# Mean over 8,192 rows: another cut of the last row group, of the early columns and of the third wide add

## The chip, the cores and the metric

The kernel runs on one core of one Trainium2 chip. The metric is the time of one execution on the device in microseconds (us), the median of several runs. A profile of one execution shows a span, from its first to its last instruction, which is somewhat shorter than that time.

## The reference

```python
def setup_inputs():
    return {"x": np.random.randn(8192, 8192).astype(np.float32)}

def reference(x):
    return np.mean(x, axis=0)
```

The input is 8,192 x 8,192 float32 values, 268 MB; the output is one row of 8,192 column means.

## The kernel before

**Row groups and strips.** The 8,192 rows are 64 groups of 128 rows, one row per SBUF partition. Since the order of rows does not matter to a sum, the groups are cut from four strips of x (`strips`, 17, 17, 15 and 15 groups), in which every partition holds consecutive rows. Two consecutive rows of a strip make a "pair", 64 KB in one run per partition, 8 MB in all; there are 30 pairs. Each strip leaves one single row group: r60, r61, r62 and r63.

**Loads.** SyncE issues every load (`load`, L52), in the order of the program. `bufs` has six slots of one row group each. Slots 4 and 5 are the accumulators `both` and `acc`: the first pair is loaded straight into them. Slots 0 to 3 take the other pairs in turn, two slots at a time (`u = (g + 2) % 4`, where g counts row groups). A load into a slot waits for the add that read the slot's earlier rows; SyncE stands at that load until then, and everything behind it stands too.

**Early columns.** A part of r60, its first six blocks of 512 columns, is loaded ahead into the tile `early` (`load_early`): two blocks as the first load of all, four blocks after the third pair. GpSimd adds them to `acc` in two instructions much later (L137, after g = 24 and g = 32), so that r60 itself is loaded without them.

**Adds.** VectorE does the summing (`add`, L80). For g = 2, 4 and 6 it does a wide add: a pair of rows is added to `both` and `acc` at once (16,384 columns). At g = 6 the wide add leaves out the first 1,024 columns of both rows (14,336 remain), and TensorE takes these instead in four products at L129, which start the accumulation in bank 0. Then `both` is added to `acc`, and from g = 8 on each pair takes two adds of 8,192: the pair's two rows into `both`, and `both` into `acc`. A no-op on ScalarE or GpSimd (L83) does each add's waiting for its load and the add ahead.

**The last groups.** VectorE adds columns 6 x 512 and up of r60 and r61, and columns 10 x 512 and up of r62, to `acc`. What is left is r61's blocks 0 to 5, r62's blocks 0 to 9, all of r63, and `acc`. These go to TensorE (`product`, L102), which multiplies each block with a column of 1/8192 and so sums over the 128 partitions. A block i of 512 columns goes to PSUM bank i // 4, column group q = i % 4 of TensorE (output partitions 32q to 32q + 31). The trace has two matmul records ("passes") for a product.

**The last quarter of the columns** (12 x 512 and up) is cut otherwise: `chunks` views its 2,048 columns as (j q w), so that a piece j holds a strip of each column group. r63 comes in four loads: blocks 0 to 7, 8 to 11, 12 to 14 and block 15 (j = 0 to 2, and j = 3). With W = 128, j = 0 to 2 make 384 columns per column group in bank 3, and j = 3 makes 128 columns in bank 4. Both the shares of `acc` and of r63 accumulate in the same bank.

**The order of the products** is the order of the list `sums`: acc 0-5, r61 0-5, r62 0-9, acc 6-7, r63 0-7, acc 8-11, r63 8-11, acc's pieces, r63's pieces. TensorE's waits come in this order.

**The output.** ScalarE copies banks 0, 1, 2 and 3 to SBUF (L182) and issues the first store, s0 (8 KB); SyncE issues s1 (16 KB, banks 1 and 2) and the last store (8 KB, tile `fin`, L199). VectorE copies bank 4 to `fin` (L192). SyncE's no-ops (`landed`, L47) wait for loads, stores and engines, since the program must not end ahead of them: some stand before s1, one before the last store, and the rest behind it.

Of the kernel before, what the change touches and what calls it, by code (L numbers as in the profile page):

```python
# [9 lines left out]
def kernel(  # L10
# [5 lines left out]
    nc = tc.nc  # L16
    f32 = mybir.dt.float32
    M, N = x.shape
    P = nc.NUM_PARTITIONS
    F = 512  # L20
    W = F // 4
    G = M // P
    U = 6
    sync = mybir.DependencyInfo(mybir.DependencyClass.Sync, mybir.DependencyReason.DATA)
# [2 lines left out]
    psp = ctx.enter_context(tc.tile_pool(name="psum", bufs=1, space=bass.MemoryType.PSUM))  # L27

    bufs = sb.tile([P, U, N], f32, name="bufs")
    both = bufs[:, U - 2, :]  # L30
    acc = bufs[:, U - 1, :]
    ones = sb.tile([P, 32], f32, name="ones")
    E = 6
    early = sb.tile([P, E * F], f32, name="early")
    fin = sb.tile([P, F], f32, name="fin")
# [2 lines left out]
    ready = sb.tile([P, 1], f32, name="ready")  # L38
    tc.keep_in_program_order(
        nc.gpsimd.tensor_add(out=ready[:], in0=ones[:, 0:1], in1=ones[:, 1:2]))  # L40
    banks = [psp.tile([P, F], f32, name=f"bank{b}") for b in range(5)]

    loads = []

    def landed(*inss):

        nop = tc.keep_in_program_order(nc.sync.nop()).ins  # L47
        for o in inss:
            tc.add_manual_dep(nop, o.name, sync, reason="SyncE waits")

    def load(dst, src):
        ins = tc.keep_in_program_order(nc.sync.dma_start(out=dst, in_=src)).ins  # L52
        k = len(loads)
        over = loads[k - 8:k - 6] if k >= 8 and k % 2 == 0 else []
        tc.declare_no_dep(ins, group="loads", keep=over, reason="the reader of the buffer waited")
        for o in over:
            tc.add_manual_dep(ins, o.name, sync, reason="covers the next load too")
        tc.add_to_no_dep_group("loads", ins)
        loads.append(ins)
        return ins  # L60
# [9 lines left out]
    def rows(g):  # L70
        return singles[g - (G - 4)]

    def load_rows(g, u, n):
        return load(bufs[:, u:u + n, :], pairs[g // 2])
# [3 lines left out]
    def add(dst, a, b, dmas):  # L78

        ins = tc.keep_in_program_order(nc.vector.tensor_add(out=dst, in0=a, in1=b)).ins  # L80
        if dmas:
            waiter = nc.scalar if len(adds) % 8 > 1 else nc.gpsimd
            nop = joins[waiter] = tc.keep_in_program_order(waiter.nop()).ins  # L83
            for o in dmas + adds[-1:]:
                tc.add_manual_dep(nop, o.name, sync, reason="the no-op waits")
            for group in ("loads", "adds"):
                tc.declare_no_dep(ins, group=group, reason="the no-op waited")
            tc.add_manual_dep(ins, nop.name, sync, reason="waits for both at once")
        elif adds:
            tc.declare_no_dep(ins, group="loads", reason="the add ahead waited")  # L90
        tc.declare_no_dep(ins, group="early", reason="the no-op waited, or the add behind it")
        tc.add_to_no_dep_group("adds", ins)
        adds.append(ins)

    def load_early(lo, hi):
        load(early[:, lo * F:hi * F], rows(G - 4)[:, lo * F:hi * F])

    def product(b, q, cols, start, stop):
        dst = banks[b][32 * q:32 * q + 32, :]
        if b > 2:  # L100
            dst = dst.rearrange("p (j w) -> p j w", w=W)[:, :cols.shape[1], :]
        return tc.keep_in_program_order(nc.tensor.matmul(  # L102
            out=dst,
            lhsT=ones[:],
            rhs=cols,
            start=start,
            stop=stop,
            tile_position=(0, 32 * q),
            skip_group_check=True,
        )).ins  # L110

    sums2 = bufs[:, U - 2:, :]
    load_early(0, 2)
    first = [load_rows(0, U - 2, 2)]
    tc.keep_in_program_order(nc.scalar.copy(out=warm[:], in_=ones[:]))  # L115
    ahead = []
    for g in range(2, G - 4, 2):
        u = (g + 2) % 4
        dma = load_rows(g, u, 2)
        if g < 8:  # L120
            cols = slice(0 if g < 6 else 2 * F, N)
            add(sums2[:, :, cols], sums2[:, :, cols], bufs[:, u:u + 2, cols], [dma] + first)
            first = []
            if g == 4:
                load_early(2, E)
            if g == 6:
                for q in range(2):
                    for j in range(2):
                        product(0, q, bufs[:, u + j, q * F:(q + 1) * F], j == 0, False)  # L129
                add(acc, acc, both, [])  # L130
            continue
        add(both, bufs[:, u, :], bufs[:, u + 1, :], [dma])
        add(acc, acc, both, ahead)
        ahead = []
        if g in (24, 32):
            cols = slice(0, 2 * F) if g == 24 else slice(2 * F, E * F)
            ins = tc.keep_in_program_order(nc.gpsimd.tensor_add(  # L137
                out=acc[:, cols], in0=acc[:, cols], in1=early[:, cols])).ins
            tc.add_to_no_dep_group("early", ins)
            ahead = [joined] = [ins]  # L140

    r60, r61, r62, r63 = [bufs[:, (G - 4 + 2 + j) % 4, :] for j in range(4)]
    cols = slice(E * F, N)
# [3 lines left out]
    dma = load(r62, rows(G - 2))  # L147
    cols = slice(10 * F, N)
    add(acc[:, cols], acc[:, cols], r62[:, cols], [dma])
    for lo, hi in [(0, 8), (8, 12), (12, 15), (15, 16)]:  # L150
        load(r63[:, lo * F:hi * F], rows(G - 1)[:, lo * F:hi * F])

    sums = []

    def blocks(row, lo, hi):
        for i in range(lo, hi):
            sums.append((i // 4, i % 4, row[:, i * F:(i + 1) * F]))

    def chunks(row, lo, hi):
        for q in range(4):  # L160
            cols = row[:, 12 * F:].rearrange("p (j q w) -> p q j w", j=4, q=4)[:, q, lo:hi, :]
            sums.append((3 + lo // 3, q, cols))

    blocks(acc, 0, 6)
    blocks(r61, 0, 6)
    blocks(r62, 0, 10)
    blocks(acc, 6, 8)
    blocks(r63, 0, 8)
    blocks(acc, 8, 12)
    blocks(r63, 8, 12)  # L170
    chunks(acc, 0, 3)
    chunks(acc, 3, 4)
    chunks(r63, 0, 3)
    chunks(r63, 3, 4)
    for n, (b, q, cols) in enumerate(sums):
        summed = product(b, q, cols, all(k[:2] != (b, q) for k in [(0, 0), (0, 1)] + sums[:n]),
                         all(k[:2] != (b, q) for k in sums[n + 1:]))

    res = both[:, :3 * F].rearrange("p (b c) -> p b c", b=3)
# [1 line left out]
    def copy(dst, src):  # L181
        return tc.keep_in_program_order(nc.scalar.copy(out=dst, in_=src)).ins  # L182

    def store(engine, dst, src):
        return tc.keep_in_program_order(engine.dma_start(out=dst, in_=src)).ins

    copy(res[:, 0, :], banks[0][:])
    s0 = store(nc.scalar, out[:4 * F].rearrange("(q c) -> q c", q=4), res[0:P:32, 0, :])
    for b in (1, 2):
        copy(res[:, b, :], banks[b][:])  # L190
    copied = copy(fin[:, :3 * W], banks[3][:, :3 * W])
    ended = nc.vector.tensor_copy(out=fin[:, 3 * W:], in_=banks[4][:, :W]).ins  # L192
    landed(*joins.values())
    landed(loads[-6])
    landed(*loads[-5:-3])
    landed(joined)
    s1 = store(nc.sync, out[4 * F:12 * F].rearrange("(b q c) -> q b c", q=4, c=F), res[0:P:32, 1:3, :])
    landed(copied)
    ins = store(nc.sync, out[12 * F:].rearrange("(j q w) -> q j w", j=4, q=4),  # L199
          fin[0:P:32, :].rearrange("q (j w) -> q j w", w=W))  # L200
    tc.declare_no_dep(ins, copied, reason="the no-op waited")
    landed(*loads[-3:-1])
    landed(loads[-1], s0)
    landed(s1, summed)
    landed(ended)
    hold = tc.keep_in_program_order(nc.vector.nop()).ins
    tc.add_manual_dep(hold, s1.name, sync, reason="VectorE ends late")
# [30 lines left out]
```

## Time and profile before

| | us |
|---|---|
| median of 3 runs | 628.55 |
| lowest and highest run | 628.15, 629.1 |
| span of the profiled execution | 626.3 |
| the profiled execution's own total time | not given by the profile |
| median less span | 2.3 |
| VectorE busy (60 instructions) | 527.7 |
| TensorE matmuls busy (120 records) | 18.3 |
| GpSimd busy | 7.4 |
| ScalarE busy | 3.7 |
| HBM read | 268.44 MB, 429 GB/s over the span |

The page of the profile gives busy time by engine (PE is TensorE, PEld its weight loads, DVE VectorE, ACT ScalarE, POOL GpSimd, SP SyncE; a "q" behind a name is the engine's sequencer), then the share of time in which the transfer engines were busy, then groups of instructions by line with the mean duration of one. The chain of waits follows the work back from what ended last. The timeline lists instructions by start and duration, and in brackets how long the engine had been idle and what ended it. Windows give the busy time of each engine in a stretch of the span, with the DMA share and GB/s. Beside these views, the trace holds a record of each DMA packet (start, duration, size) and of each semaphore update, by which the end and the landing of a load can be told apart. All times count from the span's start.

| group of instructions | count | mean ns of one |
|---|---|---|
| VectorE add, 8,192 columns | 53 | 8,745 |
| VectorE add, 16,384 columns | 2 | 17,225 |
| VectorE add, 14,336 columns | 1 | 15,093 |
| TensorE matmul record, 512 columns | 88 | 725 |
| TensorE matmul record, 384 columns | 16 | 492 |
| TensorE matmul record, 128 columns | 16 | 273 |
| ScalarE copy from PSUM, 512 columns | 3 | 586 |
| ScalarE copy from PSUM, 384 columns | 1 | 480 |
| VectorE copy from PSUM, 128 columns | 1 | 292 |

Matmul records overlap, so the mean of one is more than the time by which it moves the next.

### The profile page before, as it was taken

The numbers are of one execution on the slowest core, as the hardware profiler recorded it, in microseconds if no ns is written. First come the engines' busy times: TensorE is split into PE (matmuls) and PEld (weight loads), VectorE is DVE, ScalarE is ACT, GpSimd is POOL, SyncE is SP. The second block draws the span as 40 slices with busy tenths as digits, with TensorE's granted clock in tenths as the row PEclk, the third lists the DMA queues.
The fourth block names the chain that finished last, engine by engine and source line by source line (L and its number), as shares of the span: only waits on it lengthen the run. The fifth ranks groups of instructions, "written<-read, shape, count | busy, mean of one in ns | idle before, by whom it ended". The sixth has DMA issues, their size and how long they took to land.

```text
span 626.3 us, 464 instructions
## 1 busy us (share of the span) xinstructions
PE 18.3 (3%) x120; PEld 4.6 (1%) x120; DVE 527.7 (84%) x60; ACT 3.7 (1%) x6; POOL 7.4 (1%) x8
## 2 busy tenths in 40 slices
PE   0000020000000000000000000000000000000035
PEld 0000000000000000000000000000000000000001
DVE  0028979999988998888988899988898888998895
ACT  0000000000000000000000000000000000000001
POOL 0000000000000000010000200000000000000000
PEclk9999999999999999999999999999999999999999
DMA  9999999999999999999999999999999999999997
GB/s 393 444 402 434 437 469 402 469 402 465 406 448 423 440 431 423 448 410 460 406 465 402 469 402 469 402 469 402 469 402 465 406 448 423 423 448 406 431 435 305
DMA packets 5658, 268.50 MB, mean 429 GB/s; under 512 B 636, under 2 KB 652, under 8 KB 1048
## 3 DMA queue, kind: packets, MB, share of 16 engines
q1 hardware_dynamic: 5648, 268.46, 99.2%
q8 instruction: 1, 0.02, 0.0%
q10 hardware_dynamic: 8, 0.01, 0.0%
q14 instruction: 1, 0.01, 0.0%
HBM read 268.44 MB, written 0.03 MB: 429 GB/s over the span
## 4 chain that ended last, share of the span: by engine, by line
DMA 70%; DVE 28%; PE 1%; SPq 0%; issue 0%; ACTq 0%; POOLq 0%
DMA bufs<-in_x_dram 70%; DVE bufs L80 28%; PE bank L102 1%; SPq L52 0%; ACTq L83 0%; DVE fin L192 0%; POOLq L83 0%
## 5 line engine op out<-in xcount | busy, mean ns | idle before, releaser
L80 DVE TENSOR_TENSOR bufs<-bufs 128x8192 f32<-128x8192 f32 (+4 forms) x59 | 527.4, 8939 | 92.2 <-POOLq L83 52.3
L102 PE MATMUL bank<-bufs,ones 128*32 128x512 f32 (+2 forms) x120 | 18.3, 634 | 605.0 <-DVE bufs L80 517.7
L137 POOL TENSOR_TENSOR bufs<-bufs,early 128x1024 f32<-128x1024 f32 (+1 forms) x2 | 6.8, 3416 | 350.0 <-DVE bufs L80 350.0
L102 PEld LDWEIGHTS bank<-bufs,ones 128*32 128x32 f32 x120 | 4.6, 120 | 618.5 <-issue 610.7
L182 ACT COPY bufs<-bank 128x512 f32<-128x512 f32 x3 | 1.8, 586 | 618.2 <-PE bank L102 618.2
L192 DVE COPY fin<-bank 128x128 f32<-128x128 f32 x1 | 0.3, 292 | 3.8 <-PE bank L102 3.8
L115 ACT ACT_TABLE_LOAD x1 | 1.3, 1283 | 0.7 <-PEq L222 0.7
L182 ACT COPY fin<-bank 128x384 f32<-128x384 f32 x1 | 0.5, 480 | 1.0 <-PE bank L102 1.0
L115 ACT COPY warm<-ones 128x32 f32<-128x32 f32 x1 | 0.2, 217 | 0.0
L40 POOL TENSOR_TENSOR ready<-ones 128x1 f32<-128x1 f32 x1 | 0.2, 192 | 0.1
L37 POOL MEMSET ones<- 128x32 f32 x1 | 0.1, 124 | 0.3 <-POOLq L222 0.3
L222 POOL MEMSET const-bfloat16-1.0<- 128x1 bf16 x1 | 0.1, 101 | 0.0
L222 POOL MEMSET const-uint8-127<- 128x1 uint8 x1 | 0.1, 101 | 0.0
L222 POOL MEMSET const-float32-0.0<- 128x1 f32 x1 | 0.1, 98 | 0.2 <-issue 0.2
L222 POOL MEMSET const-float32-1.0<- 128x1 f32 x1 | 0.1, 98 | 0.0
## 6 DMA issues: line engine op xcount, KB each, us to landing
bufs<-in_x_dram SPq DMA_DIRECT2D x2, 4096.0 KB, 16.7
bufs<-in_x_dram SPq DMA_DIRECT2D x1, 2560.0 KB
bufs<-in_x_dram SPq DMA_DIRECT2D x1, 2048.0 KB, 21.3
early<-in_x_dram SPq DMA_DIRECT2D x1, 1024.0 KB, 62.0
bufs<-in_x_dram SPq DMA_DIRECT2D x1, 1024.0 KB, 23.2
bufs<-in_x_dram SPq DMA_DIRECT2D x1, 768.0 KB, 24.7
early<-in_x_dram SPq DMA_DIRECT2D x1, 512.0 KB
bufs<-in_x_dram SPq DMA_DIRECT2D x30, 29.9
```

Of the source, the lines that this page charges most:

```text
L37: nc.gpsimd.memset(ones[:], 1.0 / M)
L40: nc.gpsimd.tensor_add(out=ready[:], in0=ones[:, 0:1], in1=ones[:, 1:2]))
L80: ins = tc.keep_in_program_order(nc.vector.tensor_add(out=dst, in0=a, in1=b)).ins
L102: return tc.keep_in_program_order(nc.tensor.matmul(out=dst, lhsT=ones[:], rhs=cols, start=start, stop=stop, tile_position=(0, 32 * q), ski ...
L115: tc.keep_in_program_order(nc.scalar.copy(out=warm[:], in_=ones[:]))
L137: ins = tc.keep_in_program_order(nc.gpsimd.tensor_add(out=acc[:, cols], in0=acc[:, cols], in1=early[:, cols])).ins
L182: return tc.keep_in_program_order(nc.scalar.copy(out=dst, in_=src)).ins
L192: ended = nc.vector.tensor_copy(out=fin[:, 3 * W:], in_=banks[4][:, :W]).ins
L222: nc = _bacc.Bacc("TRN2", target_bir_lowering=False, num_devices=1)
```

## The change

It has three parts.

1. The early columns are loaded as three blocks first of all and three after the third pair, instead of two and four. GpSimd's adds stay as they are.
2. The third wide add (g = 6) covers all 16,384 columns; the four products on that pair's first columns go, and bank 0 starts with acc's products.
3. r63 is loaded in five parts instead of four: 8, 4, 2.5, 1 and 0.5 blocks. W is 64, so the last quarter has eight pieces j. acc's and r63's pieces 0 to 4 (320 columns) accumulate in bank 3. acc's pieces 5 to 7 (192 columns) go to bank 4 by themselves, and VectorE copies them to `fin`. r63's pieces 5 and 6 (128 columns) go to bank 5 and its piece 7 (64 columns) to bank 6, and VectorE adds each bank to its part of `fin`. In the list of products, acc's blocks 8 and 9 move ahead of r63's first eight, and acc's pieces 5 to 7 ahead of acc's blocks 10 and 11. The last store writes runs of 64 values instead of 128. SyncE has one no-op more behind it.

```diff
-    W = F // 4
+    W = F // 8
...
-    banks = [psp.tile([P, F], f32, name=f"bank{b}") for b in range(5)]
+    banks = [psp.tile([P, F], f32, name=f"bank{b}") for b in range(7)]
...
-    load_early(0, 2)
+    load_early(0, E // 2)
...
         if g < 8:
-            cols = slice(0 if g < 6 else 2 * F, N)
-            add(sums2[:, :, cols], sums2[:, :, cols], bufs[:, u:u + 2, cols], [dma] + first)
+            add(sums2[:], sums2[:], bufs[:, u:u + 2, :], [dma] + first)
             first = []
             if g == 4:
-                load_early(2, E)
+                load_early(E // 2, E)
             if g == 6:
-                for q in range(2):
-                    for j in range(2):
-                        product(0, q, bufs[:, u + j, q * F:(q + 1) * F], j == 0, False)
                 add(acc, acc, both, [])
...
-    for lo, hi in [(0, 8), (8, 12), (12, 15), (15, 16)]:
-        load(r63[:, lo * F:hi * F], rows(G - 1)[:, lo * F:hi * F])
+    for lo, hi in [(0, 16), (16, 24), (24, 29), (29, 31), (31, 32)]:
+        cols = slice(lo * F // 2, hi * F // 2)
+        load(r63[:, cols], rows(G - 1)[:, cols])
...
-    def chunks(row, lo, hi):
+    def chunks(row, b, lo, hi):
         for q in range(4):
-            cols = row[:, 12 * F:].rearrange("p (j q w) -> p q j w", j=4, q=4)[:, q, lo:hi, :]
-            sums.append((3 + lo // 3, q, cols))
+            cols = row[:, 12 * F:].rearrange("p (j q w) -> p q j w", j=8, q=4)[:, q, lo:hi, :]
+            sums.append((b, q, cols))
...
-    blocks(acc, 6, 8)
+    blocks(acc, 6, 10)
     blocks(r63, 0, 8)
-    blocks(acc, 8, 12)
+    chunks(acc, 4, 5, 8)
+    blocks(acc, 10, 12)
     blocks(r63, 8, 12)
-    chunks(acc, 0, 3)
-    chunks(acc, 3, 4)
-    chunks(r63, 0, 3)
-    chunks(r63, 3, 4)
+    chunks(acc, 3, 0, 5)
+    chunks(r63, 3, 0, 5)
+    chunks(r63, 5, 5, 7)
+    chunks(r63, 6, 7, 8)
...
-    copied = copy(fin[:, :3 * W], banks[3][:, :3 * W])
-    ended = nc.vector.tensor_copy(out=fin[:, 3 * W:], in_=banks[4][:, :W]).ins
+    copied = copy(fin[:, :5 * W], banks[3][:, :5 * W])
+    nc.vector.tensor_copy(out=fin[:, 5 * W:], in_=banks[4][:, :3 * W])
+    for b, cols in [(5, slice(5 * W, 7 * W)), (6, slice(7 * W, 8 * W))]:
+        ended = tc.keep_in_program_order(nc.vector.tensor_add(
+            out=fin[:, cols], in0=banks[b][:, :cols.stop - cols.start], in1=fin[:, cols])).ins
...
-    ins = store(nc.sync, out[12 * F:].rearrange("(j q w) -> q j w", j=4, q=4),
+    ins = store(nc.sync, out[12 * F:].rearrange("(j q w) -> q j w", j=8, q=4),
           fin[0:P:32, :].rearrange("q (j w) -> q j w", w=W))
...
-    landed(*loads[-3:-1])
-    landed(loads[-1], s0)
-    landed(s1, summed)
+    landed(*loads[-4:-2])
+    landed(*loads[-2:])
+    landed(s0, s1)
+    landed(summed)
     landed(ended)
```

More of the change, by code (lines that the diff above doesn't have):

```diff
@@ L166 @@
     blocks(r62, 0, 10)
-    blocks(acc, 6, 8)
+    blocks(acc, 6, 10)
     blocks(r63, 0, 8)
-    blocks(acc, 8, 12)
+    chunks(acc, 4, 5, 8)
+    blocks(acc, 10, 12)
     blocks(r63, 8, 12)
-    chunks(acc, 0, 3)
-    chunks(acc, 3, 4)
-    chunks(r63, 0, 3)
-    chunks(r63, 3, 4)
+    chunks(acc, 3, 0, 5)
+    chunks(r63, 3, 0, 5)
+    chunks(r63, 5, 5, 7)
+    chunks(r63, 6, 7, 8)
     for n, (b, q, cols) in enumerate(sums):
-        summed = product(b, q, cols, all(k[:2] != (b, q) for k in [(0, 0), (0, 1)] + sums[:n]),
+        summed = product(b, q, cols, all(k[:2] != (b, q) for k in sums[:n]),
                          all(k[:2] != (b, q) for k in sums[n + 1:]))
@@ L190 @@
         copy(res[:, b, :], banks[b][:])
-    copied = copy(fin[:, :3 * W], banks[3][:, :3 * W])
-    ended = nc.vector.tensor_copy(out=fin[:, 3 * W:], in_=banks[4][:, :W]).ins
+    copied = copy(fin[:, :5 * W], banks[3][:, :5 * W])
[3 more added lines that the diff above has]
+            out=fin[:, cols], in0=banks[b][:, :cols.stop - cols.start], in1=fin[:, cols])).ins
     landed(*joins.values())
-    landed(loads[-6])
-    landed(*loads[-5:-3])
+    landed(loads[-7])
+    landed(*loads[-6:-4])
     landed(joined)
```

## The prediction, made before the changed kernel was run

> **What bounds the kernel now.** I read the page first: the share of the DMA queue and the slices of DMA, then busy time in chosen windows.
>
> ```profile
> span 626.3 us, 464 instructions
> ...
> DMA  9999999999999999999999999999999999999997
> ...
> q1 hardware_dynamic: 5648, 268.46, 99.2%
> ```
>
> ```profile
> 110.00:600.00 490.00, 0.00 (x0) 0.00 (x0) 447.86 (x52) 0.00 (x0) 6.83 (x2) 1.00 1.00 433
> 617.90:622.50 4.60, 4.57 (x52) 1.61 (x56) 1.70 (x1) 1.76 (x3) 0.00 (x0) 1.00 0.95 383
> 622.50:626.30 3.80, 0.87 (x16) 0.17 (x8) 0.29 (x1) 0.48 (x1) 0.00 (x0) 0.94 0.03 9
> ```
>
> The last two figures of a window are the DMA share and GB/s. The transfer engines are full (1.00) in the bulk and nearly empty (0.03) after 622.5. In the packet records of the trace the first load packet starts at 1.77 us and the last ends at 622.46, and less than 0.4 us of 16 engines' time is missing between. So the span is 1.8 us of start, 620.7 us of full queue and 3.8 us of tail. All bytes still have to be read, so an edit counts only if it opens a hole in the queue, changes the packets' own time, or changes the tail. The chain of waits puts 70% on DMA, but it follows VectorE from 84 to 134 us, so I looked there for queue holes:
>
> ```profile
> 60.11 23.90 DMA bufs<-in_x_dram
> 84.01 0.04 ACTq L83
> 84.05 0.02 issue
> 84.07 15.10 DVE bufs L80
> 99.17 0.02 issue
> 99.20 8.70 DVE bufs L80
> ```
>
> Here the third wide add (15.10 us) starts as soon as its rows land at 84.01. Its end at 99.17 frees the slot into which SyncE then loads (issue at 99.25, 0.33 long). The timeline of the tail shows the rest:
>
> ```profile
> 617.93 5.44 PE L102 MATMUL bank<-bufs,ones 128*32 128x512 f32 x64 [0.68 <-DMA bufs<-in_x_dram]
> ...
> 622.24 0.70 SPq L185 DMA_DIRECT2D out_dram<-bufs  x1
> 622.93 0.17 PEld L102 LDWEIGHTS bank<-bufs,ones 128*32 128x32 f32 x8 [0.47 <-DMA bufs<-in_x_dram]
> 623.22 0.48 ACT L182 COPY fin<-bank 128x384 f32<-128x384 f32 x1 [1.00 <-PE bank L102]
> 623.44 0.29 DVE L192 COPY fin<-bank 128x128 f32<-128x128 f32 x1 [3.84 <-PE bank L102]
> 623.77 0.54 SPq L185 DMA_DIRECT2D out_dram<-fin  x1
> ```
>
> TensorE runs as one piece from the landing of r63's first part (617.88) to 623.37, although the last part lands only at 622.88. So it is behind its data, and **the tail is set as much by TensorE's backlog as by the last byte**. Then VectorE copies (to 623.73), ScalarE ends almost together (623.70), SyncE issues until 624.31, and the store lands at 625.48.
>
> **The change, part by part.** The sum is made against this execution's 626.26 us; the profile gives no total for it, so I add the difference to the median of the runs, 628.55 (2.3 us outside the span).
>
> *Early blocks 3+3.* Bytes and issues (0.39 and 0.44 us, at the start) stay. Packets of 4,096 and 8,192 bytes become two of 6,144. Packet records have medians of 159, 309 and 237 ns, and each engine moves 8 of each: 8 x (2 x 237 - 468) = +0.05 us for all that follows. The first wide add starts 0.6 us later (8 x (237 - 159)), as does the issue behind it (60.11). The engines have work until 64.0 in the packet records, so that is covered.
>
> *Third wide add whole.* The rows of 16,384 took 17.23 us, this one 15.09: +2.13 on VectorE. The four products at 84 us go (8 records, 3.63 us of TensorE); TensorE idles there, so nothing is gained. The load behind the add is issued at 84.12 + 17.23 = 101.37 instead of 99.25, until 101.70. From the end of an issue to its first packet I find 0.64 us (early load: 1.13 to 1.77) and 0.65 (last store: 624.31 to 624.96), and 0.43 more until all 16 engines had one at the start: 102.34 to 102.77. The load in flight ends on the first engine at 102.70 and on the last at 103.03, plus 0.05. Every engine then has the next packet 0.3 us before it runs dry; cost 0, against 2.4 us of cover before. The other loads behind VectorE are safer: that at 116.71 goes to 118.9, and the queue lasts to 122.1. VectorE, 2.2 us late, regains 1.9 us in every period of two row groups, by its idle time at 181 us (1.94), and is level before 200 us.
>
> *Last group as five parts.* 128 more packets, 8 per engine, plus one more completion packet. Packet time is 8 to 10 ns plus size over 27 GB/s (2,048 bytes: 84 ns; 6,144: 237), so the parts cost 8 x (198 + 84 + 47) against 8 x (237 + 84): +0.06, and 0.01 for the completion. With the early 0.05 the last landing goes from 622.88 to 623.00. Its issue (0.33 to 0.43 us near 598.5) lies 19 us ahead of SyncE's next wait.
>
> *TensorE's backlog.* A pass of 512 columns takes 0.43 us (weight loads at 618.38, 618.81, 619.24), every product is two passes, and the four column groups run side by side. After 617.93 groups 2 and 3 keep all their columns: two of r63's blocks 0-7 and block 10 or 11 of both acc and r63 (eight passes), then 2 x (192 + 320 + 320 + 128 + 64) columns instead of 2 x (384 + 128 + 384 + 128). The total is the same. Moving acc's blocks 8 and 9 ahead relieves groups 0 and 1 alone. With the +0.05, TensorE reaches the last part at 623.04; it landed at 623.00 and the step from landing to matmul is 0.045 (617.88 to 617.93). So the last products start at 623.05 instead of 622.97, take 2 x 0.054 instead of 2 x 0.109, and are complete near 623.34 instead of 623.37. The smaller last part gains 0.03 us, not what its size suggests.
>
> *The two adds.* No row shows VectorE adding from PSUM. Rows nearby: COPY from PSUM of 128 columns 292 ns; adds in SBUF 3,357 (3,072 columns) and 8,692 (8,192), which is 156 ns plus 1.042 per column. I take 290 ns for 128 columns and 223 for 64. Bounds: 133 and 67 without any fixed part, and twice the value above. The copy of 192 columns (some 0.36 us near 620.2) is done long before. The penultimate products run 622.83 to 623.05 and are complete at 623.23; VectorE starts 0.07 later, as it did (623.37 to 623.44), and ends at 623.59. **The last add, ready at 623.41, is queued behind it**: 623.62 to 623.84, instead of 623.73. So +0.11. If two adds overlapped, the end would be 623.63, 0.10 earlier than before; the bounds above put it between 623.50 and 624.36.
> VectorE's steady adds never overlap: one ends at 99.16 and the next starts at 99.20, but that one waits for the first. The Trainium skill ("VectorE: DVE Perf Modes", section "The DRAIN you can't avoid") says that the pipeline empties after every operation and that leaving semaphores out does not avoid it. By that rule the end is the 623.84 that I take, not 623.63; no pair of independent adds in this trace tests it.
>
> *ScalarE and SyncE.* Bank 3 is ready 0.2 us earlier and its copy has 320 columns (by 586 ns for 512 and 480 for 384: 0.43): done at 623.5, so it stops being a co-limit. Bank 2 is ready 0.4 us later; the 16 KB store issues near 622.6 to 623.3, still ahead of 623.84, and lands near 624.6, ahead of 625.5. If that cover went, its issue (0.70) would delay the last one. The extra no-op behind the last store (0.06 each) waits under the store's flight.
>
> *The last store* writes 32 runs of 256 bytes instead of 16 of 512, on four engines: 512-byte packets took 27 ns; by the line above 256 bytes take 18, so 8 x 18 against 4 x 27 is +0.04. The issue (0.54) I leave; rows of issues run from 0.33 to 1.07.
>
> **Sum**: VectorE's end +0.11, store +0.04, together +0.15: 628.55 + 0.15 = **628.7 us**.
>
> **The rivals.**
> 1. *The adds overlap or are shorter* (the size split pays): 628.55 - 0.10 + 0.04 = 628.5. ScalarE's early end speaks for it, VectorE's in-order rows against.
> 2. *The queue runs dry at 102 us* (slower). Place: the load at 101.37. It decides once an issue needs more than about 1 us from its end to its first packet. The 8 KB store from ScalarE, issued until 620.75 among loads, had its first packet at 622.04: 1.29 us. Then packets start at 102.99 to 103.42, 0.3 us late, and a first packet meets an empty pipe (the longest 64 KB packet took 2.88 against 2.42: 0.46). All of it reaches the end, since no later slack exists: 628.7 + 0.8 = 629.5. At 1.8 us of delay it passes 629.8. Against it: that store shared its engines with full load queues; the 0.64 and 0.65 rows are those of empty ones.
> 3. *The last store's short runs cost more.* If each 256-byte write is a read and a write, 8 packets take up to 54 ns (0.43 against 0.11), and a further trip like that from its last packet to its landing (625.15 to 625.48) comes on top: +0.65, 629.3. No row has 256-byte writes, so nothing speaks for or against beyond 512-byte packets lying on the line.
> The Trainium skill ("DMA: Bandwidth & Descriptors", section "Specifications") gives 512 bytes as the least for line rate and a read-modify-write below; by it this rival happens, and no run so far shows its price.
> 4. *The change moves nothing* since bytes and TensorE columns are equal: 628.55, inside the forecast.
>
> **How the numbers follow.** About 0.2%, 1.26 us, is what a measurement of this kernel can tell from no change. Forecast (with rival 4) 0.60; rival 1 0.13; rival 2 0.14, of which 0.06 passes 629.8; rival 3 0.10, of which 0.02 passes it; something before the first packet or outside the span that gains over 1.26 us 0.03. Faster 0.03, slower 0.08, same 0.89. The range: below, 623.50 for VectorE (-0.23) and the spread of the runs (628.15 is 0.4 below the median), so 628.0; above, 624.36 for VectorE (629.2) and rival 2 by its row, 629.6.
>
> **What would show it.** The last landing near 623.0; TensorE one piece from 617.98 to 623.34; two VectorE adds touching, ending near 623.84; DMA share still 1.00 around 103 us and the pair load's landings 0.05 later than before (a jump of 0.3 or more there is rival 2); the last store's landing 1.7 us after its issue starts (2.3 is rival 3). I would be wrong if landings drift through the bulk, which nothing in the change explains.

## The result, and the profile after

The changed kernel takes 630.16 us (median of 5 runs, 629.98 to 631.02) against 628.46 us (628.15 to 629.1) for the kernel before, measured with it: a ratio of 1.0033, 95% interval 1.0021 to 1.0045. It is 1.7 us slower, where 628.7 had been forecast, and above the range. The profiled execution took 630.12 us with a span of 628.0, against 626.3 before.

The page after, in the same lines as before:

```profile
span 628.0 us, 467 instructions
...
DMA  9999999999999999999999999999999999999996
...
q1 hardware_dynamic: 5808, 268.46, 99.0%
```

The transfer engines still look full, and the bytes are the same. A mean over 16 engines and slices of 16 us hides what happened; the chain of waits after shows it (start, duration, what):

```profile
60.91 23.21 DMA bufs<-in_x_dram
84.13 0.03 ACTq L83
84.16 0.02 issue
84.18 17.24 DVE bufs L80
101.42 0.02 issue
101.44 8.70 DVE bufs L80
...
136.47 26.99 DMA bufs<-in_x_dram
163.47 0.03 ACTq L83
```

and, of the chain before, the two lines that answer to the last two:

```profile
134.22 27.50 DMA bufs<-in_x_dram
161.72 0.03 ACTq L83
```

The load that goes into the slot of the third wide add is issued 2.19 us later. SyncE's lines, of the kernel before and then of the changed one:

```profile
99.25 0.33 SPq L52 DMA_DIRECT2D bufs<-in_x_dram  x1
```

```profile
101.44 0.33 SPq L52 DMA_DIRECT2D bufs<-in_x_dram  x1
```

In the chains, a load has landed where a DMA piece ends. The load that landed at 84.01 now lands at 84.13 (+0.12). The one that landed at 161.72 now lands at 163.47: **+1.75 us, lost between 84 and 162 us and never regained** (the chains have landings at 587.46 before and 589.23 after, +1.77). The tail gives a little back: from the last landing to the end of the span it was 626.26 - 622.88 = 3.38 us and is 627.98 - 624.72 = 3.26.

The window from 60 to 140 us, of the kernel before and then of the changed one (the last two figures are the DMA share and GB/s):

```profile
60.00:140.00 80.00, 3.63 (x8) 0.66 (x8) 72.94 (x8) 0.00 (x0) 0.00 (x0) 1.00 1.00 433
```

```profile
60.00:140.00 80.00, 0.00 (x0) 0.00 (x0) 73.62 (x8) 0.00 (x0) 0.00 (x0) 1.00 0.99 428
```

The rate falls by 1%, but a mean over the engines does not show what sets a landing; the packet records do. They do not name the engine, so a packet that starts 2 or 3 ns behind the end of another is taken to be on the same one; the few that are left are paired so that the engine that stops last goes on first. Before, no engine idles over 0.05 us in this stretch. After, the load behind the third wide add is issued at 101.44; the load ahead of it ends on the first engine at 102.77; and three engines then stand idle for 1.30, 1.39 and 1.77 us, until 104.17, 104.18 and 104.54, while most of the others go on (two more idle there for 0.08 and 0.35). Paired the other way round, the longest of these would be 1.50 us; their sum is the same. Near 83.5, two engines idle for 0.19 and 0.41 us. In these records every engine has eight packets of 64 KB of each load, so the latest engine sets each landing from there on: on the mean, the engines end the load that lands near 162 us only 0.48 us later than before (161.62 for 161.14), but the last one ends it 1.72 us later (163.14 for 161.42).

### The profile page after: what moved, and what is told of

Its sections match the earlier page's. It is cut to its first block, busy times and chain, and to the rows that moved or that the text cites. A ratio compares the mean times of both kernels' runs of the same rounds, so it can differ in the third digit from the quotient of the medians.

```text
span 628.0 us, 467 instructions
## 1 busy us (share of the span) xinstructions
PE 14.6 (2%) x120; PEld 4.2 (1%) x120; DVE 530.3 (84%) x62; ACT 3.7 (1%) x6; POOL 7.4 (1%) x8
## 4 chain that ended last, share of the span: by engine, by line
DMA 70%; DVE 28%; PE 1%; SPq 0%; issue 0%; ACTq 0%; POOLq 0%
DMA bufs<-in_x_dram 70%; DVE bufs L80 28%; PE bank L102 1%; SPq L52 0%; ACTq L83 0%; DVE fin L192 0%; POOLq L83 0%
## 5 line engine op out<-in xcount | busy, mean ns | idle before, releaser
L80 DVE TENSOR_TENSOR bufs<-bufs 128x8192 f32<-128x8192 f32 (+3 forms) x59 | 529.5, 8975 | 91.8 <-POOLq L83 53.2
L102 PE MATMUL bank<-bufs,ones 128*32 128x512 f32 (+4 forms) x120 | 14.6, 575 | 610.5 <-DVE bufs L80 607.2
```

The source lines that it names most:

```text
L102: return tc.keep_in_program_order(nc.tensor.matmul(out=dst, lhsT=ones[:], rhs=cols, start=start, stop=stop, tile_position=(0, 32 * q), ski ...
```

## The experiments

Three theories. **1: late issue.** The whole third add frees its slot 2.1 us later, the load behind it comes too late for some engines, and only its time of issue matters. **2: the tail.** The five parts with their smaller packets cost the time. **3: the add itself.** Its width, or the products that are gone, slows transfers, whatever the time of issue. A ratio is to the kernel before, run beside it; it is not the quotient of the two medians.

### The parts by themselves

**The whole third add alone**, on the kernel before:

```diff
-            cols = slice(0 if g < 6 else 2 * F, N)
-            add(sums2[:, :, cols], sums2[:, :, cols], bufs[:, u:u + 2, cols], [dma] + first)
+            add(sums2[:], sums2[:], bufs[:, u:u + 2, :], [dma] + first)
...
-                for q in range(2):
-                    for j in range(2):
-                        product(0, q, bufs[:, u + j, q * F:(q + 1) * F], j == 0, False)
...
```

> The kernel before with the third wide add whole and its four products gone, and nothing else. Theory 1 (late issue): the load behind it is issued near 101.4 us; some engines wait 1 to 1.8 us for their first packet near 103 to 104.5 us and keep that lag to the end; 629.7 to 630.3 us. Theory 2 (the tail): 628.3 to 628.7 us, no change. Theory 3 (the add itself): 629.7 to 630.3 us.

Measured: 630.42 us against 628.37, ratio 1.0037 (1.0023 to 1.0051). The window of this kernel:

```profile
60.00:140.00 80.00, 0.00 (x0) 0.00 (x0) 73.02 (x8) 0.00 (x0) 0.00 (x0) 1.00 0.98 422
```

The issue is at 101.82, and eleven engines idle for 0.06 to 1.64 us. This part alone makes the whole loss; the tail theory falls.

**The changed kernel without it** (the narrow add and its four products put back, the reverse of the diff above):

> The changed kernel with its third wide add cut back to 14,336 columns and the four products put back; early blocks 3+3 and the five-part tail stay. Theory 1 (late issue): the load behind the third wide add is issued near 99.3 us again, 3.4 us ahead of the end of the queued load; the long holes of 1.3 to 1.8 us on three transfer engines at 103 to 104.5 us go, small ones of 0.2 to 0.4 us at 83.5 us stay because the early split still makes the load before that 0.8 us late; 628.4 to 628.9 us. Theory 2 (the tail of five parts costs the time): still 629.8 to 630.3 us. Theory 3 (the whole add itself, by its width or by the missing products, slows transfers): 628.4 to 628.9 us too.

Measured: 628.49 us, ratio 1.0001 (0.9992 to 1.0010). The issue is at 99.55; idle times are 0.23 us at 83.6 and 0.11 at 103.2, no more.

**The five-part tail alone** (the changed kernel with the narrow add, its products and the early blocks 2+4 put back):

> The kernel before with the five-part tail alone (W of 64, banks 5 and 6, the two VectorE adds, acc blocks 8 and 9 ahead); early blocks 2+4 and the narrow third wide add stay. Theory 1 (late issue): no holes beyond those of the kernel before; the tail behind the last landing is 0.1 us shorter and the last landing 0.07 later, so 628.3 to 628.6 us. Theory 2 (the tail): 629.5 us or more. Theory 3: 628.3 to 628.6 us.

Measured: 628.10 us, ratio 0.9996 (0.9987 to 1.0004). This is below what any of the theories had expected: by the medians the tail gains 0.27 us, but the interval includes no change.

**The early blocks alone:**

```diff
-    load_early(0, 2)
+    load_early(0, E // 2)
...
-                load_early(2, E)
+                load_early(E // 2, E)
```

> The kernel before with the early blocks as 3+3 and nothing else. Theory 1 (late issue): the loads behind the first two wide adds are issued 0.6 us later, near 60.8 and 80.2 us; holes of up to 0.4 us on one or two engines near 83.5 us; 628.3 to 629.0 us, at most a little slower. Theory 2 and theory 3: 628.2 to 628.6 us, no change.

Measured: 628.63 us, ratio 1.0001 (0.9993 to 1.0010), no change that can be told. The issues are at 60.97 and 80.33. No engine idles at 83 us in the profiled execution, but six packets there take 2.6 to 2.7 us instead of 2.42.

**The products taken away without lateness:**

```diff
-                for q in range(2):
-                    for j in range(2):
-                        product(0, q, bufs[:, u + j, q * F:(q + 1) * F], j == 0, False)
...
```

> The kernel before without the four products at the third wide add, which stays narrow: the first 1,024 columns of that pair of rows are left out of the sum. The load behind the add is issued near 99.2 us. Theory 1 (late issue alone): 628.1 to 628.6 us, no change. Theory 3, if the missing products slow something: 0.5 us or more slower.

Measured: 628.27 us against 628.34, ratio 0.9999 (0.9990 to 1.0008), with the issue at 99.25. Its window:

```profile
60.00:140.00 80.00, 0.00 (x0) 0.00 (x0) 73.01 (x8) 0.00 (x0) 0.00 (x0) 1.00 1.00 433
```

TensorE is as idle as after the change, and the rate is that of before: the missing products cost nothing.

### The lateness by itself

The test between theories 1 and 3 is the kernel before with nothing changed but the time of one issue. Two attempts missed. **GpSimd as the delay:**

```diff
+    nc.gpsimd.memset(fin[:], 0.0)
...
+        if g == 10:
+            for w in (F, F // 2):
+                pause = tc.keep_in_program_order(nc.gpsimd.tensor_add(
+                    out=fin[:, :w], in0=fin[:, :w], in1=fin[:, :w])).ins
+                tc.add_manual_dep(pause, adds[2].name, sync, reason="starts behind the third wide add")
         dma = load_rows(g, u, 2)
+        if g == 10:
+            tc.add_manual_dep(dma, pause.name, sync, reason="issues late")
```

> The kernel before with its narrow third wide add and its products, but the load behind them also waits for two small GpSimd adds on a tile that is idle then (512 and 256 columns, some 2.1 us), so that it is issued near 101.3 to 101.6 us while VectorE and TensorE do as before. Theory 1 (late issue): the same loss as from the whole add, 629.7 to 630.5 us, with engines idle 1 to 2 us near 103 to 105 us. Theory 3 (the whole add itself or the missing products): 628.3 to 628.7 us, no change, for neither is touched. Theory 2 (the tail): 628.3 to 628.7 us.

Measured: 645.78 us, ratio 1.0279 (1.0265 to 1.0293). The timeline of this kernel shows why:

```profile
99.50 18.49 POOL L122 TENSOR_TENSOR fin<-fin 128x512 f32<-128x512 f32 x2 [97.96 <-DVE bufs L81]
118.02 0.80 SPq L53 DMA_DIRECT2D bufs<-in_x_dram  x2
```

The two GpSimd adds, expected to take some 2 us, took 18.49, each ending about when one of VectorE's adds beside it did. The delay was 18.8 us instead of 2.1 and the loss 17.4.

**ScalarE copies in the same place** (`nc.scalar.copy(out=fin[:, :w], in_=early[:, :w])` for widths 512, 512, 512 and 256):

> The kernel before with its narrow third wide add and its products, but the load behind them also waits for four copies on ScalarE, idle then (512, 512, 512 and 256 columns into a tile unused then), which hold its issue back by 1.8 to 2.4 us, to 101.1 to 101.7 us. VectorE and TensorE do as before. Theory 1 (late issue): transfer engines idle 0.3 to 1.8 us near 103 to 104.5 us, 629.6 to 630.6 us, as with the whole add. Theory 3 (the width of the add or the missing products): 628.2 to 628.7 us, no change.

Measured: 638.50 us, ratio 1.0163 (1.0149 to 1.0177). The copies stood in ScalarE's queue behind a no-op that waited for the next add, so the issue came at 110.81, 11.6 us late; all engines idled 8.1 to 8.9 us. Neither run separates the theories, but both give the price of a queue that is wholly dry, used below.

**ScalarE copies placed right behind the third wide add**, ahead of that no-op:

```diff
         dma = load_rows(g, u, 2)
+        if g == 10:
+            tc.add_manual_dep(dma, pause.name, sync, reason="issues late")
...
             if g == 6:
...
+                for w in (F, F, F):
+                    pause = tc.keep_in_program_order(nc.scalar.copy(out=fin[:, :w], in_=early[:, :w])).ins
+                    tc.add_manual_dep(pause, adds[2].name, sync, reason="starts behind the third wide add")
                 add(acc, acc, both, [])
             continue
```

> The kernel before with its narrow third wide add and its products; right behind that add ScalarE, idle then, makes three copies of 512 columns into a tile unused then (some 0.65 us each by the run before), and the load behind the add waits for them. It is issued near 101.4 us, as with the whole add, while VectorE and TensorE do as before. Theory 1 (late issue): engines idle 0.5 to 1.8 us near 103 to 104.5 us, 629.6 to 630.6 us, as with the whole add. Theory 3 (the add's width or the missing products cost the time): 628.1 to 628.6 us, no change.

Measured: 629.16 us, ratio 1.0023 (1.0013 to 1.0032), with single runs from 628.78 to 631.95. The issue is at 101.12. In the profiled execution no engine idles, but eleven first packets take 2.6 to 3.0 us. This is less than expected; other lengths of the delay follow. **Widths 512 and 256:**

> The same with one copy of 512 and one of 256 columns: the load is issued near 100.4 us, as with one block left out of the third wide add. Theory 1 (late issue): no holes over 0.3 us, 628.1 to 628.7 us, no change. Theory 3: no change either; the run places the point from which lateness costs.

Measured: 628.89 us, ratio 1.0011 (1.0003 to 1.0020), issue at 100.36. **Widths 512, 512, 512 and 128:**

> The kernel before with the load behind the third wide add held back by ScalarE copies of 512, 512, 512 and 128 columns: issue near 101.45 us, that of the changed kernel; narrow add and products kept. Theory 1 (late issue alone): 1.2 to 2.0 us slower than before, 629.5 to 630.3 us, with some engines idle near 103 us. Theory 3 (part of the loss belongs to the whole add or to the missing products): 0.8 to 1.1 us slower, as at 101.1 us.

Measured: 631.64 us (629.95 to 631.92), ratio 1.0047 (1.0035 to 1.0060), more than either theory had expected. Of its timeline and then of its chain:

```profile
99.17 2.25 ACT L133 COPY fin<-early 128x512 f32<-128x512 f32 x4 [96.92 <-DVE bufs L80]
101.46 0.33 SPq L52 DMA_DIRECT2D bufs<-in_x_dram  x1
```

```profile
101.46 24.31 DMA bufs<-in_x_dram
...
134.55 29.88 DMA bufs<-in_x_dram
164.43 0.03 ACTq L83
```

The load issued at 101.46 becomes critical by itself (its landing, at 101.46 + 24.31, ends VectorE's wait), and the landing that was at 161.72 is at 164.43. **Four times 512:**

> The same with four copies of 512 columns: issue near 101.77 us, that of the run with the whole add alone. Theory 1 (late issue alone): 1.7 to 2.3 us slower than before, 630.0 to 630.6 us, with holes of 0.4 to 1.6 us on many engines near 103 us. Theory 3: at most 1.3 us slower.

Measured: 630.72 us, ratio 1.0038 (1.0025 to 1.0051), issue at 101.73, thirteen engines idle for 0.07 to 1.24 us.

These four kernels carry a cost of their own: their last store, issued as before, is waited for 2.2 to 2.5 us in the profiled executions instead of 1.73. An 8 KB instruction fetch starts 0.8 to 1.1 us behind the start of that store's issue in all four, against 1.6 us in the kernel before. That this fetch is the reason is argued from the times alone. So 0.4 to 0.7 us of their loss is not lateness, and the landing near 162 us, ahead of the tail, is the cleaner measure.

### More and less cover

**One block left out of the third add instead of two** (`1 * F` for `2 * F`, `range(1)` for `range(2)`):

> The kernel before with one block of 512 columns left out of the third wide add instead of two (15,360 columns, two products instead of four). The add should take 16.16 us and the load be issued near 100.3 us, half way between 99.3 and 101.4. Theory 1 (late issue): holes of at most some 0.3 to 1 us on a few transfer engines, 628.6 to 629.5 us, between the two ends. Theory 3, if the loss comes with the missing products and not with time: 628.3 us or 630.2 us, not between.

Measured: 628.24 us, ratio 1.0001 (0.9993 to 1.0010), issue at 100.28, no engine idle. Theory 1 had been given 628.6 to 629.5 us here, so its idea that the loss grows evenly with the lateness was wrong; by its time alone this run fits theory 3 as well, and it does not decide between them.

**Four blocks left out, with the five-part tail** (`4 * F`, `range(4)`):

> The kernel with the five-part tail alone, and four blocks of 512 columns left out of the third wide add instead of two (12,288 columns, eight products). The add should take 12.96 us and the load be issued near 97.2 us, over 5 us ahead of the end of the queued load. Theory 1 (late issue): no late first packets near 103 us, the spread between the first and last transfer engine stays at 0.3 to 0.4 us there; 627.7 to 628.2 us, at best 0.2 us below the tail alone, since there is little left to lose. Theory 3 (the width of the add costs time by itself): 626.5 us or less, as much below as the whole add lies above.

Measured: 628.14 us, ratio 0.9997 (0.9989 to 1.0006), issue at 97.46. More cover gains nothing more, and the gain that theory 3 asks for isn't there.

**The same with the early blocks as 1+5:**

> As the one with four blocks left out and the five-part tail, and the early columns loaded as one block first of all and five behind the third pair. The first wide add should start 0.6 us earlier and the loads behind the first two wide adds be issued near 59.6 and 78.9 us. Theory 1 (late issue): more cover at 64 and 83 us, where there is little left to lose; 627.5 to 628.2 us, the fastest of all by 0 to 0.2 us.

Measured: 628.08 us, ratio 0.9996 (0.9987 to 1.0005). This and the tail alone have the lowest medians of the study, neither clear of the kernel before.

### What follows

By the time of one issue (idle times from the packet records; the landing is the one at 161.7 before, from the profiled execution):

| kernel | issue | load ahead ends, first engine | longest idle | landing | ratio |
|---|---|---|---|---|---|
| before | 99.25 | 102.70 | none | 161.7 | 1 |
| no products | 99.25 | 102.66 | 0.25 | 161.7 | 0.9999 |
| one block out | 100.28 | 102.66 | none | 161.6 | 1.0001 |
| delay, 512 + 256 | 100.36 | 102.59 | none | 161.5 | 1.0011 |
| delay, 3 x 512 | 101.12 | 102.60 | none | 161.8 | 1.0023 |
| changed kernel | 101.44 | 102.77 | 1.77 | 163.5 | 1.0033 |
| delay, 3 x 512 + 128 | 101.46 | 102.59 | 2.49 | 164.4 | 1.0047 |
| delay, 4 x 512 | 101.73 | 102.58 | 1.24 | 163.2 | 1.0038 |
| whole add alone | 101.82 | 102.57 | 1.64 | 163.3 | 1.0037 |

With VectorE's narrow add and the products in place, a late issue alone brings the whole loss, at the same time of issue as in the changed kernel; and without products, or with an add that is one block wider, an issue in time costs nothing. (The whole add with an issue in time was not run.) Theory 1 stands. The loss does not grow evenly with the lateness. With the issue 2.2 us or more ahead of the first engine's end, holes are 0.4 us at most (and the small ones come at leads of 3 us too). At 1.5 us some executions show a loss and others don't. From 1.3 us on, single engines stand idle for 1.2 to 2.5 us. Summed over the 16 engines, the idle time near 103 us does grow: 4.9 and 3.1 us with the issue at 101.44 and 101.46, 7.9 and 7.2 at 101.73 and 101.82. But the landing goes with the latest engine and not with the sum: of these four, the kernel with the least idle time in all has the latest landing (164.4). Why a single engine idled longest at 101.46, and not at the later 101.73, is open.

## Why the prediction was wrong

**The step that failed** is the cover of the load behind the third wide add: "Every engine then has the next packet 0.3 us before it runs dry; cost 0". The chain up to it was right: the add took 17.23 us, and the issue came at 101.44 (forecast 101.37). Wrong was the term behind it, above all the 0.43 us from the first packet on any engine until all 16 had one. In the changed kernel it was at least 104.54 - 102.90 = 1.64 us (the first engine had been busy until its packet), and in the other three kernels whose engines ran dry for over 1 us at least 1.05 to 2.46. The 0.64 us from an issue's end to the first packet may have been right: with four copies of 512 it was 0.73 (102.06 to 102.79), on an engine that was busy until then. The rows of 0.64, 0.65 and 0.43 us, of the first load and the last store, are of idle queues. For a load that is issued while the engines still work on the one ahead, the last engine's first packet came 2.1 to 3.6 us after the start of the issue: 104.54 - 101.44 = 3.10 in the changed kernel, 2.40 with the whole add alone, 3.62 with the delay of 2.25 us. Besides, the margin of 0.3 us compares the last engine to be served with the last to run dry, and no row said that these are the same engine.
The Trainium skill ("DMA: Bandwidth & Descriptors", section "Latency and other measured facts") gives about 600 ns to the first byte of such a DMA. The idle queue here agrees (0.64 and 0.65 us from the issue's end), and on the busy one the 0.73 us of the first engine is not far from it; the last engine, which decided here, came 1.8 to 3.3 us after the issue's end.

**Rival 2 was the case**, with the right place and mechanism. Its condition, "more than about 1 us from its end to its first packet", was met on the five engines that stood idle (1.36 to 2.78 us; two of them lost 0.35 us at most), and its price was too small. It took 0.3 us late plus 0.46 for an empty pipe; the worst engine of the changed kernel was idle for 1.77, and its first packet took 2.87 us instead of 2.42 (+0.45). It had ended the load ahead before the last engine did, so 1.75 reached the end. Its chance, 0.14, was too low: a margin of 0.3 us had been worked out from two rows of another condition.

**The tail** had the right steps but the wrong sign. It is read from the kernel with the tail alone, whose last landing (622.89) is that of before. TensorE's last product is complete at 623.26 (forecast 623.34, with 0.05 for the early blocks). The adds take 292 and 225 ns (forecast 290 and 223). But they **overlap**, so rival 1 holds as well. The timeline merges the two, starting at 623.12:

```profile
622.90 0.42 ACT L184 COPY fin<-bank 128x320 f32<-128x320 f32 x1 [0.49 <-PE bank L102]
623.12 0.43 DVE L196 TENSOR_TENSOR fin<-bank,fin 128x128 f32<-128x128 f32 x2 [2.41 <-PE bank L102]
623.58 0.54 SPq L187 DMA_DIRECT2D out_dram<-fin  x1
```

Two adds of 292 and 225 ns fill 0.43 us: the second starts at 623.326, 0.085 us ahead of the first one's end at 623.411, as it does in the changed kernel. VectorE ends at 623.55, not at the forecast 623.84 and ahead of the 623.73 of before: -0.18 us instead of +0.11, and the span is 0.17 us shorter. The rule of the Trainium skill that the prediction leaned on ("VectorE: DVE Perf Modes", section "The DRAIN you can't avoid") does not hold for this pair, and the section itself adds that an operation which is not held starts earlier. The same page says in "Two Vector instructions with no wait between them" which instructions are held until the earlier ones have finished; the prediction had not weighed that.

**The store** with 256-byte runs costs nothing: the issue takes 0.54 us as before, its packets 18 ns each (forecast 18), and SyncE's wait ends 1.74 us after the issue starts, against 1.73. Rival 3 falls here, and with it the price of the read-modify-write that the Trainium skill's rule had suggested: no cost of it shows in these times.

**The early blocks** moved the first landings by 0.12 us (forecast 0.05) and the issues near 61 and 80 us by 0.8 (forecast 0.6). As an edit alone they are within the measurement.

## What to carry to other kernels

Where transfers bound a kernel, ask of every load how long ahead of the end of the queued work it is issued, on the engine that ends first: here 2.2 us was enough, 1.5 us only in some executions, and 1.3 us was not, and one starved engine out of 16 delays all that follows. An instruction that is off the critical path can hold the buffer that the next load needs; taking work onto it then costs at the transfer and not at the instruction. A latency that was read on an idle queue is no cover for a busy one.

## What the runs showed of the hardware that had not been expected

- A queue that has run wholly dry restarts sooner than one that is nearly dry: with the issues at 118.02 and 110.81 us, all 16 engines had their first packet within 1.24 and 1.39 us, against 2.1 to 3.6 us for the last engine in the nearly dry cases. After the dry stop each engine's first 64 KB packet took 2.8 to 3.5 us instead of 2.42.
- GpSimd's add of 512 columns took 9.47 us beside VectorE's adds (99.51 to 108.98, where VectorE's add ended at 108.08). In the kernel before, its add of 1,024 columns took 2.34 us, but VectorE was idle when that began (276.06; VectorE's next add started at 277.91).
- Two VectorE adds from PSUM without a dependency overlapped by 0.085 us. In the changed kernel the second one's product had signalled its end at 625.13, and the add started at 625.23, 0.207 us after the first one's start, as with the tail alone: it did not wait for the first one's end.
